# Buffer ownership, buffer hand-over points and pacing in a one-layer hybrid decoder trunk

## The chip, the cores and the metric

The kernel runs on one core of a Trainium2 chip. A core has a matrix engine (TensorE, PE in the profile; its weight loads are listed apart as PEld), a vector engine (DVE), a scalar engine (ACT), a general engine (POOL, GpSimd) and a sync engine (SP) that here only issues DMA transfers. Each engine runs its own instructions in order and waits on semaphores for the others. The metric is the device time of one execution in microseconds; the lower the better.

## What is computed

One decoder layer for 256 tokens of width 2048, all in 32-bit floats. The reference, cut to what matters:

```python
h = rmsnorm(x, attn_norm)
gq, gk, gv, gr, ga1, sq, sk, sv, mq, gates = split(h @ w_in)
# branch A: chunked gated linear attention, 4 heads, chunks of 64
log_a = log_sigmoid(ga1 @ w_a2 + b_a) / 16
y_gla = (rmsnorm(gla(gq, gk, gv, log_a)) * silu(gr)) @ w_br_gla
# branch B: causal stick-breaking attention, 8 heads of 128, 128-query blocks
y_sb = stick_breaking(rmsnorm(sq), rmsnorm(sk), sv) @ w_br_sb
# branch C: softmax cross-attention into 256 memory tokens, 4 heads of 256
m_k, m_v = split(rmsnorm(mem) @ w_mem_kv)
y_mem = softmax_attention(rmsnorm(mq), rmsnorm(m_k), m_v) @ w_br_mem
g = sigmoid(gates)
x = x + (g[0] * y_gla + g[1] * y_sb + g[2] * y_mem) @ w_o
gate, up = split(rmsnorm(x) @ w_gate_up)          # 2 x 5632 wide
out = x + (silu(gate) * up) @ w_down
```

## The kernel before

**Products.** Every weight matrix comes from memory in pieces of 1 MB (four 128-row slabs by 512 columns). Half a piece, called a chunk here, is split into a high and a low part: ACT rounds it to the matmul's type (`wh`, L145) and DVE subtracts to get the rest (`wl`, L146). Three matmuls per 128x128 block (high by high, high by low, low by high) then give nearly 32-bit products. A chunk is 12 full-size matmuls. `gemm` (L217 to L219) is the plain loop: 16 slabs are 8 chunks, 8 slabs are 4. `sgemm` (L256 to L259) computes two blocks of 512 columns together with a Strassen scheme on the first slabs; it also adds pieces in place, partly on DVE (L271) and partly by an accumulating DMA issued from POOL (L313, L333), and its intermediate results are copied out by ACT (L296). With p=4 it has 22 steps, of which 14 are steps of 6 matmuls and 8 are full chunks of 12; with p=2 it has 19, of which 7 have 6 matmuls and 12 have 12.

**Rings.** The 1 MB landing buffers stand in a list (`free_raw`); `loads` takes the first and the user puts it back at the end. The `wh`/`wl` buffers stand in another list (`splits`), and `parts` takes entry `turn % len(splits)`, where `turn` counts every chunk. `widen` appends a pool's buffers to both lists, `narrow` takes them out again. `ring1` lives throughout (3 landing buffers, 4 pairs of split buffers). `pre` adds one landing buffer, `ring_a` two landing buffers and two split pairs, and `ring2` three landing buffers and one split pair. `ring_a` lies where the normalised memory tokens (pool `mems`) were; `ring2` and `mrg` lie where the pools of the linear attention (`gl`, `att`, `sec`) were.

**Background.** Work that is not a product is written as generators in the list `background`. After each chunk a product calls `step`, which runs the first generator to its next `yield`; `flush` runs all that is left. `pipelined` makes such a generator from stages of several heads: in round r it runs the last stage for head r-2, the middle one for r-1 and the first for r, with a `yield` after each. The program order written down so is then the priority of a planner: on each engine the instruction that is ready first by the planner's own costs goes first, and program order decides between ready ones. The planner also chooses which of a tag's buffers a tile gets.

**The order of the stages.** Memory keys and values (four `gemm`s on `w_mem_kv`); `mq` in two `gemm`s of 512 columns; `sq`, `sk`, `sv` by `sgemm`, with the memory heads (`m_scores`, `m_turn`, `m_out`) in the background of `sq`; `gqk` and `gv` by `sgemm` with p=2, with the stick-breaking heads (`s_scores`, `s_rest`, `s_out`) in the background; `gr`, an `sgemm` whose result goes through a sigmoid; the small decay projection `w_ga`; then four rounds of a gate `gemm`, its sigmoid, the memory branch's product and `merge`, with the linear attention `gla` in the background; then the other two branches, `w_o` and the feed-forward part.

**Staged outputs.** The heads' results leave through `put_out` (L634 to L640): ACT copies PSUM into a tile of tag `rb`, which has two buffers and also holds the softmax's transposed scores (`m_turn`, L689) and the stick-breaking heads' `nl` (L760), and ACT's queue issues the store. `fetch_out` (L642) reads a whole branch back (1 MB) and splits it into `oh`, `ol` tiles (two steps, each with one split of 1024 columns).

Of the kernel before, what the change touches and what calls it, by code (L numbers as in the profile page):

```python
# [16 lines left out]
P = 128  # L17
# [60 lines left out]
def trunk(ctx: ExitStack, tc: tile.TileContext, a, out):  # L78
# [11 lines left out]
    def widen(name, raw, w, side="right"):  # L90

        pool = tc.alloc_tile_pool(name=name, bufs=1, side=side, reuse_waits="tile")
        free_raw.extend([(pool, raw)] * raw)
        splits.extend([(pool, w)] * w)
        return pool
# [20 lines left out]
    def tmp():  # L116
        return ps.tile([P, NB], F32, tag="tmp", name="tmp", bufs=4)
# [11 lines left out]
    def flush():  # L129
        while background:  # L130
            step()

    def pipelined(stages, n, gap):

        for r in range(n + gap * (len(stages) - 1)):
            for i in reversed(range(len(stages))):
                j = r - gap * i
                if 0 <= j < n:
                    stages[i](j)
                    yield  # L140

    def split(hi, lo, src, scale=None):

        if scale is None:
            act.copy(hi, src)  # L145
            dve.tensor_tensor(lo, src, hi.bitcast(F32), op=ALU.subtract)  # L146
        else:
            act.activation(hi, src, AF.Copy, scale=scale)
            dve.scalar_tensor_tensor(lo, src, scale, hi.bitcast(F32), op0=ALU.mult, op1=ALU.subtract)
# [19 lines left out]
    def loads():  # L169

        slot = pool, bufs = free_raw.pop(0)
        return pool.tile([P, KG, NB], F32, tag="raw", name="raw", bufs=bufs), lambda: free_raw.append(slot)

    def parts():

        turn[0] += 1
        pool, n = splits[turn[0] % len(splits)]
        return [pool.tile([P, IT], F32R, tag=f"w{x}", name=f"w{x}", bufs=n) for x in "hl"]
# [300 lines left out]
    def project(dst, xs, w, c0, rstd):  # L479
        for n in range(0, MIX, NB):  # L480
            evac(dst[:, :, n : n + NB], gemm(xs, w, c0 + n), rstd)
# [128 lines left out]

    pre = widen("pre", 1, 0, "left")
    opool.release()
    ring_a = widen("ring_a", 2, 2)

    def ring(tag, bufs, dtype=F32):
        return att.tile([P, NB], dtype, tag=tag, name=tag, bufs=bufs)
# [4 lines left out]
    def rb():  # L621
        return ring("rb", 2)
# [11 lines left out]

    def put_out(o, c, src):

        n = src.shape[1] // T
        v = rb()[:, : n * T]
        act.copy(v, src)
        nc.scalar.dma_start(o[:, c : c + n], v.rearrange("p (c t) -> p c t", c=n))  # L640

    def fetch_out(o):  # L642
        high, low = outT()

        def work():
            raw, done = loads()
            v = raw[:].rearrange("p g n -> p (g n)").rearrange("p (c t) -> p c t", c=8)
            nc.sync.dma_start(v, o[:])
            yield
            for c in range(0, 8, 4):  # L650
                split(high[:, c : c + 4], low[:, c : c + 4], v[:, c : c + 4])
                if c == 4:
                    done()
                yield

        background.append(work())
        return high, low
# [52 lines left out]

    sx = make_forms([xtiles], form_tiles())
    mq = section("mq", "d")
    project(mq, xs, w_in, O_MQ, r_x)
    flush()
    background.append(normed_T(mqT, mq, MH, MD, g_mq, ra))
    background.append(pipelined((m_scores, m_turn, m_out), MH, 1))
# [64 lines left out]
        put_out(od_sb, h, o[:, :T])  # L781

    flush()
    background.append(pipelined((s_scores, s_rest, s_out), SH, 1))
    gqk, gv = section("gqk", "a"), section("gv", "d")
    wide(gqk, O_GQ, 2)
    wide(gv, O_GV, 2)
# [9 lines left out]
            dve.tensor_tensor(v, v, sg, op=ALU.mult)  # L797
    narrow(ring_a)
    opool = tc.alloc_tile_pool(name="opool", bufs=4, side="right", reuse_waits="tile")
    o_mem, o_sb = fetch_out(od_mem), fetch_out(od_sb)  # L800


    narrow(pre)
    gl = tc.alloc_tile_pool(name="gl", bufs=1, reuse_waits="tile")
    raw, done = loads()
    raw = raw[:].rearrange("p g n -> p (g n)").rearrange("p (k n) -> p k n", k=KD)
    nc.sync.dma_start(raw, a["w_ga"])
    p = tmp()
    for k0 in range(0, KD, 8):
        hi, lo = (x[:].rearrange("p (k n) -> p k n", k=8) for x in parts())  # L810
        split(hi, lo, raw[:, k0 : k0 + 8])
        if k0 == 8:
            done()
        for j in range(8):
            xh, xl = xs[k0 + j]
            pe.matmul(p[:, :T], hi[:, j], xh, start=k0 + j == 0, stop=False)
            pe.matmul(p[:, :T], hi[:, j], xl, start=False, stop=False)
            pe.matmul(p[:, :T], lo[:, j], xh, start=False, stop=k0 + j == KD - 1)
    gaT = gl.tile([GR, T], F32, name="gaT", bufs=1)
    dve.tensor_copy(gaT[:], p[:GR, :T])  # L820
    flush()

    def gate():
        return piece()[:] if kit is not None else gl.tile([P, NB], F32, tag="sg", name="sg", bufs=2)[:]
# [112 lines left out]
                    )  # L937
                    yield

    background.append(gla())  # L940

    def to_chunks(src, n, hi, lo, gain):

# [31 lines left out]

    xo = pairs(o_mem)
    for n in range(0, D, NB):
        if n + NB == D:

            flush()  # L980
            gl.release()
            att.release()
            sec.release()
            ring2 = widen("ring2", 3, 1, "left")
            kit = mrg = tc.alloc_tile_pool(name="mrg", bufs=1, reuse_waits="tile")
        g = gemm(xs, w_in, O_G + n)
        sg = [gate() for _ in range(2)]
        for t in range(2):
            sigmoid(sg[t], g[t][:], t, False)
        merge(sg, gemm(xo, a["w_br_mem"], n), n, True)  # L990
# [170 lines left out]
```

## Time and profile before

| | us |
|---|---|
| median of 3 runs | 1655.15 |
| the runs | 1655.0, 1655.15, 1659.49 |
| the profiled execution | 1657.52 |
| its span, first to last instruction | 1655.7 |
| PE busy (share) | 1633.6 (99%) |
| DVE busy | 1308.4 (79%) |
| ACT busy | 1012.6 (61%) |

The span is what the trace covers; the profiled execution's own time is 1.8 us longer. A busy PE is not PE at its peak: the ends of matmuls are modelled, and the mean TensorE clock that was granted (0.994 over the span) is given by stretch. The profile's parts used here are the waits (who waited for whom, and how long), the busy times by stretch, the instructions in order of time, the groups by line, and the DMA transfers with the time from issue to landing.

### The profile page before, as it was taken

The page shows a single profiled execution, that of the slowest core. Times are in us where ns is not written, and L with a number is a line of the kernel's source. Part 1 is how long each engine was busy: PE and PEld are TensorE (multiplying, and loading weights), DVE is VectorE, ACT ScalarE, POOL GpSimd, SP SyncE. Part 2 cuts the span into 40 slices and gives each one's busy share as a digit, 9 for nine tenths or more (in the row PEclk, how much of TensorE's full clock was granted, in tenths as well). Part 3 has the DMA queues.
Part 4 walks back from the last instruction along what each step waited for, and adds up shares of the span by engine and source line. Part 5 has one row for each costly group of instructions (what it writes and reads, how often), then busy time and mean ns, then how long its engine had stood idle before and what let it go on. Part 6 is the DMA issues. An engine that isn't in the chain of part 4 may idle for free.

```text
span 1655.7 us, 19396 instructions
## 1 busy us (share of the span) xinstructions
PE 1633.6 (99%) x7290; PEld 1333.5 (81%) x7290; DVE 1308.4 (79%) x1506; ACT 1012.6 (61%) x1229; POOL 62.9 (4%) x81
## 2 busy tenths in 40 slices
PE   8999989999999999999999999999999999999999
PEld 6878878878887778888888888888888888888887
DVE  5857778877766557777787799999878999888994
ACT  6755566765745347556565666666666666666662
POOL 0000000000000000000000000000110000110000
PEclk9999999999999999999999999999999999999999
DMA  8785657657563367578585858787887687887792
GB/s 318 287 311 156 220 189 237 191 171 245 186 208 130 127 248 275 178 272 259 167 280 176 276 177 274 211 279 250 275 255 250 205 278 253 272 257 246 210 342 88
DMA packets 63006, 381.93 MB, mean 231 GB/s; under 512 B 6944, under 2 KB 12576, under 8 KB 19264
## 3 DMA queue, kind: packets, MB, share of 16 engines
q1 hardware_dynamic: 50256, 322.26, 51.7%
q0 software_dynamic: 10288, 55.58, 17.7%
q10 hardware_dynamic: 2368, 2.85, 0.5%
q8 instruction: 57, 0.93, 0.2%
q14 instruction: 37, 0.30, 0.1%
HBM read 322.99 MB, written 10.49 MB: 201 GB/s over the span
## 4 chain that ended last, share of the span: by engine, by line
PE 87%; DVE 3%; ACT 2%; DMA 1%; issue 1%; DVEq 0%; ACTq 0%
PE acc L256 17%; PE acc L259 17%; PE acc L258 16%; PE acc L218 6%; PE acc L219 6%; PE acc L217 6%; PE tmp L259 5%; PE tmp L256 5%; PE tmp L258 5%; PE tmp L435 2%; DVE wl L146 1%; ACT wh L145 1%; DMA od_mem<-rb 1%; PE tmp L904 0%; DMA od_sb<-rb 0%
## 5 line engine op out<-in xcount | busy, mean ns | idle before, releaser
L146 DVE TENSOR_TENSOR wl<-raw,wh 128x1024 fp32r<-128x1024 f32 (+1 forms) x740 | 891.7, 1219 | 274.2 <-ACT wh L145 261.4
L145 ACT CAST wh<-raw 128x1024 fp32r<-128x1024 f32 (+1 forms) x740 | 772.4, 1051 | 533.3 <-PE acc L259 247.1
L256 PE MATMUL acc<-wh,hh 128*128 128x512 f32 x452 | 178.8, 395 | 0.0
L258 PE MATMUL acc<-wl,hh 128*128 128x512 f32 x452 | 176.0, 389 | 0.0
L259 PE MATMUL acc<-wh,hl 128*128 128x512 f32 x452 | 175.4, 390 | 0.0
L256 PE MATMUL acc<-wh,xTh 128*128 128x512 f32 x424 | 170.1, 401 | 4.8 <-ACT acc L296 4.8
L258 PE MATMUL acc<-wl,xTh 128*128 128x512 f32 x424 | 166.7, 393 | 0.0
L259 PE MATMUL acc<-wh,xTl 128*128 128x512 f32 x424 | 166.0, 394 | 0.0
L271 DVE TENSOR_TENSOR raw<-raw 128x1024 f32<-128x1024 f32 x114 | 138.2, 1218 | 0.8
L217 PE MATMUL acc<-wh,oh 128*128 128x512 f32 x320 | 125.5, 394 | 1.9 <-ACT wh L145 1.1
L218 PE MATMUL acc<-wl,oh 128*128 128x512 f32 x320 | 124.9, 390 | 1.7 <-DVE wl L146 1.7
L219 PE MATMUL acc<-wh,ol 128*128 128x512 f32 x320 | 124.8, 390 | 0.0
L256 PEld LDWEIGHTS acc<-wh,hh 128*128 128x128 f32 x452 | 84.9, 188 | 18.4 <-ACT acc L296 1.0
L256 PEld LDWEIGHTS acc<-wh,xTh 128*128 128x128 f32 x424 | 80.3, 189 | 23.6 <-ACT acc L296 7.9
L259 PEld LDWEIGHTS acc<-wh,hl 128*128 128x128 f32 x452 | 84.8, 188 | 17.9
L258 PEld LDWEIGHTS acc<-wl,hh 128*128 128x128 f32 x452 | 85.0, 188 | 16.8
L256 PE MATMUL tmp<-wh,sh 128*128 128x512 f32 x246 | 97.3, 395 | 0.0
L259 PE MATMUL tmp<-wh,sl 128*128 128x512 f32 x246 | 96.0, 390 | 0.0
L258 PE MATMUL tmp<-wl,sh 128*128 128x512 f32 x246 | 95.8, 389 | 0.0
L259 PEld LDWEIGHTS acc<-wh,xTl 128*128 128x128 f32 x424 | 80.3, 189 | 17.0
L258 PEld LDWEIGHTS acc<-wl,xTh 128*128 128x128 f32 x424 | 80.4, 190 | 15.5
L217 PE MATMUL acc<-wh,xTh 128*128 128x512 f32 x192 | 76.7, 402 | 4.2 <-ACT wh L145 4.2
(313 smaller groups left out, 2526.4 us busy)
## 6 DMA issues: line engine op xcount, KB each, us to landing
raw<-in_w_gate_up SPq DMA_DIRECT2D x88, 1024.0 KB, 6.0
raw<-in_w_in SPq DMA_DIRECT2D x72, 1024.0 KB, 5.0
raw<-in_w_down SPq DMA_DIRECT2D x44, 1024.0 KB, 7.2
raw<-raw POOLq DMA_DIRECT2D x41, 1024.0 KB, 7.9
raw<-in_w_gate SPq DMA_DIRECT2D x32, 1024.0 KB, 5.9
raw<-in_w_o SPq DMA_DIRECT2D x16, 1024.0 KB, 5.3
raw<-in_w_mem_kv SPq DMA_DIRECT2D x15, 1024.0 KB, 5.0
raw<-in_w_br_mem SPq DMA_DIRECT2D x8, 1024.0 KB, 5.0
```

The costliest lines, as they stand in the source:

```text
L145: act.copy(hi, src)
L146: dve.tensor_tensor(lo, src, hi.bitcast(F32), op=ALU.subtract)
L217: pe.matmul(o[t][:], xh[:, s], wh[:, j], start=k == 0, stop=False)
L218: pe.matmul(o[t][:], xh[:, s], wl[:, j], start=False, stop=False)
L219: pe.matmul(o[t][:], xl[:, s], wh[:, j], start=False, stop=k == nk - 1)
L256: pe.matmul(dst[:], xh, wh, start=id(dst) not in begun, stop=False, skip_group_check=True)
L258: pe.matmul(dst[:], xh, wl, start=False, stop=False, skip_group_check=True)
L259: pe.matmul(dst[:], xl, wh, start=False, stop=last, skip_group_check=True)
L271: dve.tensor_tensor(x, x, y, op=ALU.add)
L435: pe.transpose(dst, src, ident)
```

## The change

Five things are edited; the arithmetic stays the same.

1. `put_out` gets its own tag `out` with two buffers of 256 columns. A memory head's result of 512 columns is copied and stored in two halves (8 copies and stores in place of 4); a stick-breaking head's in one, as before.
2. `ring_a` is made between the two halves of the `mq` projection, not before the first.
3. The stick-breaking heads get one empty step at the end of each round.
4. The linear attention's generator is made before the `w_ga` projection and its first step (two small loads) is run there. The read-back of the memory branch is put in the background behind `w_ga`, ahead of the rest of the linear attention, in place of both branches' read-backs before `w_ga` and a `flush` behind it.
5. In the last of the four gate rounds the gate's `gemm` comes first, and then the flush, the release of `gl`, `att` and `sec`, and the making of `ring2` and `mrg`. The read-back of the stick-breaking branch is started there.

```diff
-    def pipelined(stages, n, gap):
+    def pipelined(stages, n, gap, pause=False):
...
                     stages[i](j)
                     yield
+            if pause:
+                yield
...
     pre = widen("pre", 1, 0, "left")
     opool.release()
-    ring_a = widen("ring_a", 2, 2)
...
     def put_out(o, c, src):
 
-        n = src.shape[1] // T
-        v = rb()[:, : n * T]
-        act.copy(v, src)
-        nc.scalar.dma_start(o[:, c : c + n], v.rearrange("p (c t) -> p c t", c=n))
+        for i in range(src.shape[1] // T):
+            v = att.tile([P, T], F32, name="out", tag="out", bufs=2)
+            act.copy(v[:], src[:, i * T : (i + 1) * T])
+            nc.scalar.dma_start(o[:, c + i], v[:])
...
-    project(mq, xs, w_in, O_MQ, r_x)
+    evac(mq[:, :, :NB], gemm(xs, w_in, O_MQ), r_x)
+    ring_a = widen("ring_a", 2, 2)
+    evac(mq[:, :, NB:], gemm(xs, w_in, O_MQ + NB), r_x)
...
-    background.append(pipelined((s_scores, s_rest, s_out), SH, 1))
+    background.append(pipelined((s_scores, s_rest, s_out), SH, 1, True))
...
-    o_mem, o_sb = fetch_out(od_mem), fetch_out(od_sb)
...
-    (the w_ga projection, and gaT)
-    flush()
...
-    background.append(gla())
+    steps = gla()
+    next(steps)
+
+    (the w_ga projection, and gaT)
+    o_mem = fetch_out(od_mem)
+    background.append(steps)
...
     for n in range(0, D, NB):
+        g = gemm(xs, w_in, O_G + n)
         if n + NB == D:
 
             flush()
...
             ring2 = widen("ring2", 3, 1, "left")
             kit = mrg = tc.alloc_tile_pool(name="mrg", bufs=1, reuse_waits="tile")
-        g = gemm(xs, w_in, O_G + n)
+            o_sb = fetch_out(od_sb)
         sg = [gate() for _ in range(2)]
```

The two lines in brackets stand for the same lines, moved and not altered.

More of the change, by code (lines that the diff above doesn't have):

```diff
@@ L799, in trunk @@
     opool = tc.alloc_tile_pool(name="opool", bufs=4, side="right", reuse_waits="tile")
-    o_mem, o_sb = fetch_out(od_mem), fetch_out(od_sb)
     narrow(pre)
     gl = tc.alloc_tile_pool(name="gl", bufs=1, reuse_waits="tile")
[L805 to L820, printed above, removed]
-    flush()
     def gate():
@@ L938, in gla_T @@
                     yield
-    background.append(gla())
+    steps = gla()
+    next(steps)
+    raw, done = loads()
+    raw = raw[:].rearrange("p g n -> p (g n)").rearrange("p (k n) -> p k n", k=KD)
+    nc.sync.dma_start(raw, a["w_ga"])
+    p = tmp()
+    for k0 in range(0, KD, 8):
+        hi, lo = (x[:].rearrange("p (k n) -> p k n", k=8) for x in parts())
+        split(hi, lo, raw[:, k0 : k0 + 8])
+        if k0 == 8:
+            done()
+        for j in range(8):
+            xh, xl = xs[k0 + j]
+            pe.matmul(p[:, :T], hi[:, j], xh, start=k0 + j == 0, stop=False)
+            pe.matmul(p[:, :T], hi[:, j], xl, start=False, stop=False)
+            pe.matmul(p[:, :T], lo[:, j], xh, start=False, stop=k0 + j == KD - 1)
+    gaT = gl.tile([GR, T], F32, name="gaT", bufs=1)
+    dve.tensor_copy(gaT[:], p[:GR, :T])
+    o_mem = fetch_out(od_mem)
+    background.append(steps)
     def to_chunks(src, n, hi, lo, gain):
```

## The prediction

> **What bounds the kernel now.** I read the page's busy times, then the waits of PE, then the busy times by stretch around those waits, then the instructions in order of time on the engines that PE waited for.
>
> ```profile
> span 1655.7 us, 19396 instructions
> PE 1633.6 (99%) x7290; PEld 1333.5 (81%) x7290; DVE 1308.4 (79%) x1506; ACT 1012.6 (61%) x1229; POOL 62.9 (4%) x81
> ...
> PE acc L217 <- ACT wh L145: 5.3, 3, 2.1
> PE acc L256 <- ACT acc L296: 4.8, 2, 4.5
> PE acc L218 <- DVE wl L146: 3.4, 6, 0.9
> PE tmp L779 <- DVE ra L774: 1.6, 1, 1.6
> ...
> L146 DVE TENSOR_TENSOR wl<-raw,wh 128x1024 fp32r<-128x1024 f32 (+1 forms) x740 | 891.7, 1219 | 274.2 <-ACT wh L145 261.4
> L145 ACT CAST wh<-raw 128x1024 fp32r<-128x1024 f32 (+1 forms) x740 | 772.4, 1051 | 533.3 <-PE acc L259 247.1
> ```
>
> PE bounds the kernel, and the edits take no matmul away. All that can be won is where PE waited (1655.7 - 1633.6 = 22.1 us) and where its clock was low. The rows by stretch (columns: stretch, its length, PE busy and matmuls, PEld, DVE, ACT, POOL, then granted clock, DMA share, GB/s) price the places:
>
> ```profile
> 95.00:105.00 10.00, 7.39 (x32) 5.48 (x31) 6.76 (x11) 6.94 (x8) 0.00 (x0) 1.00 0.86 342
> 205.00:225.00 20.00, 15.53 (x56) 12.21 (x56) 12.15 (x21) 10.97 (x15) 0.00 (x0) 0.83 0.33 122
> 330.00:340.00 10.00, 8.43 (x40) 6.59 (x39) 7.42 (x13) 7.00 (x12) 0.00 (x0) 1.00 0.88 317
> 445.00:460.00 15.00, 14.22 (x72) 11.40 (x72) 12.33 (x17) 12.79 (x20) 0.00 (x0) 0.89 0.76 259
> 575.00:592.00 17.00, 14.05 (x49) 10.77 (x48) 10.13 (x14) 4.92 (x6) 0.00 (x0) 0.80 0.75 304
> 700.00:1000.00 300.00, 300.00 (x1353) 247.70 (x1352) 242.47 (x275) 176.79 (x212) 11.88 (x17) 1.00 0.69 232
> ```
>
> The waits list who waited for whom (total, times, longest); the two groups give one split of a chunk, 1.05 on ACT and 1.22 on DVE. The last row by stretch is undisturbed: a chunk of 12 matmuls is 12 x 300/1353 = 2.7 us. In the others, idle is length less PE busy, and the loss by the clock is length times (1 - clock). A: 10 - 7.39 = 2.6 us. B: 4.5 + 20 x 0.17 = 7.9, less some 0.4, an estimate, for low clock that began before PE's wait ended, 7.5. C: 1.6. D: 0.8 + 15 x 0.11 = 2.4. E: 2.95 + 17 x 0.20 = 6.35, less the same 0.4, 6.0. Together 20.1 us; each edit has one of these places as its own.
>
> **Edit 2, `ring_a` one block on (place A).** Chunks are counted by `turn`: the memory projections use 33 (their first `gemm` begins with pieces of 1, 1 and 2 slabs, so 9, then three times 8). The first chunk of `mq` is number 34. With `ring_a` in the list there are 6 entries, and 34 mod 6 = 4 is `ring_a`'s, whose place is free only when the last memory product has read it. In order of time (start, duration, engine, line, idle before it and who ended that):
>
> ```profile
> 97.19 2.00 ACT L145 CAST wh<-raw 128x1024 fp32r<-128x1024 f32 x2 [4.60 <-DMA raw<-in_w_in]
> 99.09 1.26 ACT L477 ACTIVATE mv_mqT<-acc,r_mem 128x512 f32<-128x512 f32 x2
> 100.24 3.89 ACT L145 CAST wh<-raw 128x1024 fp32r<-128x1024 f32 x4
> ```
>
> Two later chunks are rounded at 97.19; the first comes after the evacuation, at 100.24, and PE waits for it. With the list of four, 34 mod 4 = 2 is a `ring1` buffer, and ACT sat idle for 4.60 us before 97.19. The second block starts at 42 mod 6 = 0, a `ring1` buffer, and reaches `ring_a` 4 chunks later, at least 4 + 8 chunks after it came free. What is late next is the landing of the pieces: those two chunks themselves waited for a DMA until 97.19, some 1.9 us before PE needs the first (100.24 + 3.89/4, less the 2.1 that PE waited), against 1.05 and 1.22 for a split. I take -2.6; bounds -2.6 and 0.
>
> **Edit 5, the pools behind the last gate (place E).** `turn` goes on: 16 for `mq`, 22 each for `sq`, `sk`, `sv`, 19 each for `gqk`, `gv`, 22 for `gr`, 2 for `w_ga`, three rounds of 8 + 4. The last gate's first chunk is number 214. With `ring2` there are 5 entries and 214 mod 5 = 4 is `ring2`'s, in memory that the linear attention holds until its last operation (L920, which reads `gr`):
>
> ```profile
> 578.96 1.21 DVE L920 TENSOR_TENSOR g_og<-g_og,gr 128x1024 f32<-128x1024 f32 x1
> ...
> 579.45 1.99 ACT L145 CAST wh<-raw 128x1024 fp32r<-128x1024 f32 x2 [1.66 <-PE acc L219]
> ...
> 581.50 0.73 PE L217 MATMUL acc<-wh,xTh 128*128 128x512 f32 x2 [2.08 <-ACT wh L145]
> 583.10 0.80 PE L218 MATMUL acc<-wl,xTh 128*128 128x512 f32 x1 [0.87 <-DVE wl L146]
> ```
>
> The second of the two casts at 579.45 starts when L920 ends (580.17); PE starts when it ends. Moved, the last gate runs on `ring1` alone like the three gates before it, in which PE shows no such wait, and its 8 chunks (some 21 us) lie between L920 and the first use of `ring2`. The linear attention ends two steps later than now (three steps of read-back ahead of it, one of its own already done), so L920 comes up to 5.4 us later, still inside that cover. It then falls among the last gate's first subtractions on DVE (1.2 each), whose chunks are split ahead of PE. The read-back of `od_sb` moves into the last branch product: 2 casts and 2 subtractions of 1.0 and 1.2, hidden by its 4 chunks; without that cover 2.4 us. `ring2`'s landing buffers join a gate later, so loads of the next gate weights run less far ahead: 0 to +3. I take -6.0; bounds -6.3 and -1.
>
> **Edit 4, `w_ga` and the read-backs (place D).**
>
> ```profile
> 424.77 0.33 SPq L648 DMA_DIRECT2D raw<-od_mem  x1
> 435.76 0.33 SPq L648 DMA_DIRECT2D raw<-od_sb  x1
> ...
> 440.22 3.90 ACT L145 CAST oh<-raw 128x1024 fp32r<-128x1024 f32 x4 [2.54 <-PE acc L259]
> ...
> 450.24 1.03 ACT L145 CAST wh<-raw 128x1024 fp32r<-128x1024 f32 x1
> ...
> 450.52 1.12 PE L837 MATMUL tmp<-rb,gaT 16*128 16x512 f32 x2 [0.51 <-DVE gaT L820]
> ```
>
> SP now issues both read-backs ahead of the first gate's pieces, and ACT rounds `oh` from 440.22 to 444.1; the first gate's first cast comes behind `gr`'s sigmoid at 450.24, when PE has nothing left of `w_ga`. Afterwards the first gate piece is issued where `od_mem` stands (424.77), and its cast fits into the ACT time that `oh` has now; the second buffer pair is free when `gr`'s last chunk ends. `od_mem` takes the second issue and is split in steps 2 and 3. The decay's first matmuls (L837) no longer stand between `w_ga` and the gate: their 1.1 us are moved, not saved. What is late next is the second chunk, behind the same sigmoid. I take -2.0; bounds -2.4 and +2 (if the cast stays behind the sigmoid, PE lacks the 1.1 us that it fills now, and the low clock of that place, 15 x 0.11, stays or grows).
>
> **Edits 1 and 3, the stick-breaking heads (place C).** Where `nl` got the buffer of a store in flight, DVE waited 2.0 us and PE 1.6:
>
> ```profile
> DVE rb L760 <- DMA od_sb<-rb: 2.0, 1, 2.0
> ...
> od_sb<-rb ACTq DMA_DIRECT2D x8, 128.0 KB, 2.7
> ```
>
> With its own two buffers a store has two rounds to land, 17 us at the 8.6 us between issues (312.8 to 373.3 for 8, in the rows by tile below), against 6.6 at worst. `nl` never meets a store. The 10 empty steps bring 24 steps to 34; the two projections give 2 x 19 = 38, so all stay covered. -1.6; bounds -2.5 (ACT's crowding where `gqk` is evacuated) and +0.5 where the heads' end now meets `gv`'s evacuation.
>
> **Edit 1, the memory heads (place B).** Here I expect little.
>
> ```profile
> L640 ACTq DMA_DIRECT2D od_mem<-rb x4: 326/334/353, 178.5 to 208.6; - x4
> ...
> DMA to landing us min/median/max: 2.5/5.7/9.1
> ...
> L640 ACTq DMA_DIRECT2D od_sb<-rb x8: 326/326/1954, 312.8 to 373.3; - x8
> ...
> DMA to landing us min/median/max: 1.9/2.7/6.6
> ...
> 197.46 0.85 POOL L333 DMA_DIRECT2D raw<-raw  x1 [35.90 <-DVE ra L680]
> ...
> 208.02 0.58 ACT L639 COPY rb<-tmp 128x512 f32<-128x512 f32 x1 [5.15 <-DMA od_mem<-rb]
> 213.81 0.57 ACT L296 COPY acc<-tmp 128x512 f32<-128x512 f32 x1
> 214.44 0.80 PE L256 MATMUL acc<-wh,xTh 128*128 128x512 f32 x1 [4.47 <-ACT acc L296]
> ```
>
> The last head's copy waits for the store before it (issued 198.84, landed 9.1 us later, behind the 1 MB accumulating transfer issued at 197.46); ACT stands, and its queue holds up the casts and the copy L296 for which PE waits. Two buffers for two halves of each head is the same distance as before: the first half still waits for the head before it. The store is no smaller in all, only cut, and ACT issues 0.33 us more and starts one more copy per head, hidden but at the last. Bounds: halves that land like `od_sb`'s median, 2.7, would take the stall away (-7.5); a second half that lands behind a further load costs up to about +2.5. I take +0.5, since the row nearest is the 9.1 of this very store.
>
> The Trainium skill, page "DMA: Bandwidth & Descriptors", section "Anatomy of one DMA — SWDGE (gpsimd) path", speaks against the cut too: a transfer has a fixed part of about 2.0 us that does not scale with its size, so halving 256 KB saves only some 0.3 us by its formula, an estimate. The trace's medians, 5.7 against 2.7, fall by more, but in other stretches; by the page's figure place B would come out at +0.2.
>
> **The sum.** -2.6 - 6.0 - 2.0 - 1.6 + 0.5 = -11.7. The profiled execution took 1657.5 (its span and 1.8 us around it), which becomes 1645.8; it stood 2.4 above the median of the runs, 1655.15, from which I go: 1643.5.
>
> **Rivals.**
>
> *The store stall goes as well.* The planner may give the halves their buffers otherwise, or the shift of everything by A's 2.6 us may part the store from the accumulating transfer. For it: the four stores' landings spread from 2.5 to 9.1. Against it: the accumulation and the store hang on the same heads' steps. 1643.5 - 0.5 - 7.5 = 1635.5.
>
> *New lateness eats half.* Loads that run less far ahead behind `ring2` (+3), the cast behind the sigmoid (+4 against my term) and the ends of the heads (+2): up to 9, say half, 1648. For it: the chunks before the last gate are split only when PE frees a buffer (1.66 before 579.45).
>
> *The low clock has another cause.* If it does not come from PE's idle time, the low clock at D and E stays: 15 x 0.11 + 17 x 0.20 - 0.4 = 4.6, so 1648. For it: 2.6 us of idle at A left the clock at 1.00, while 0.8 at D went with 0.89. Against it: outside these stretches the clock is 1.00 where PE is never idle. The Trainium skill, page "TensorE: Matmul & The Clock Gate", section "What's actually happening", lowers the clock after an idle window of some 3.4 us; by that rule only B's wait would bring a low clock, and D and E agree with it badly.
>
> *It does not do what it says.* The planner orders by readiness, so each wait could come back one block on: 1655. Against it: the buffers have been free for whole blocks by then.
>
> *Slower: the paced heads outrun their cover.* If the two projections had fewer than 34 steps, the rest would run in the flush with nothing beside it.
>
> ```profile
> L756 ACT ACTIVATE ra<-tmp 128x384 f32<-128x384 f32 x8 | 3.8, 481 | 0.4 <-PE tmp L754 0.4
> ...
> L760 DVE SCALAR_TENSOR_TENSOR rb<-tmp,ra 128x384 f32<-128x384 f32 x8 | 4.4, 554 | 2.8 <-DMA od_sb<-rb 2.0 <-ACT ra L758 0.9
> L772 DVE TENSOR_TENSOR ra<-ra,tmp 128x384 f32<-128x384 f32 x8 | 4.4, 552 | 5.0 <-PE tmp L771 5.0
> ```
>
> The first stage of a head is a chain of four such ACT and four DVE operations, about 4 x 0.5 + 4 x 0.5 + 0.6 on PE = 4.6; ten steps are 2.5 rounds, 11.5; the last head's two other stages some 4, and a low clock behind it like B's 3.4: +19, or 1662.5. It decides from the 35th step that is needed; I count 38 there.
>
> **How the numbers follow.** My forecast 0.48, with 1639 to 1648 as its own range; the store stall gone 0.18; new lateness 0.14; the clock 0.06; nothing changed 0.08; slower 0.06. About 0.3%, 5 us, is what a measurement of this kernel can tell from no change. Faster: 0.48 + 0.18 + 0.14 + 0.06 = 0.86; within 0.08; slower 0.06. The range 1634 to 1651 takes in the first four cases.
>
> **What would show it.** Right: no wait of L217 near 99 and 579 us, and clock 1.00 at D and E; DVE L760 never released by a store; a copy L639 in `mq`'s heads still released by `od_mem`, with L296 and a low clock behind it. Wrong: a new wait of PE on `wh` or `wl` at the second `mq` block, the last branch product or the end of `gv`; or a trace in which L639 waits for no store.

## The result, and the profile after

The changed kernel takes 1637.38 us (median of 4 runs, 1636.86 to 1638.47), the kernel before beside it 1655.08 (1654.84 to 1659.49). The ratio is 0.9888 with a 95% interval of 0.987 to 0.9905: faster by 17.7 us, where the prediction had 11.7 and 1643.5. The time lies in the predicted range, below the likeliest case's own range (1639 to 1648) and next to the rival in which the store stall goes as well (1635.5).

Line numbers are 2 to 4 higher now: the splits are L148 and L149, the products L220 to L222 and L259 to L262, the copy out of `sgemm` L299, `put_out` L641 and L642. The linear attention's are 16 lower: its last operation, L920 before, is L904. First the page of the kernel after, span and busy times.

```profile
span 1634.9 us, 19398 instructions
PE 1625.0 (99%) x7290; PEld 1330.8 (81%) x7290; DVE 1308.6 (80%) x1506; ACT 1014.5 (62%) x1233; POOL 62.9 (4%) x81
```

The span is 20.8 us shorter, but PE's waits shrank only from 22.1 to 9.9 us. The rest is PE busy time, 8.6 us less for the same 7290 matmuls: they ran at a higher clock or back to back. So the busy times by stretch have to say where the time came from. Before:

```profile
0.00:90.00 90.00, 85.21 (x368) 66.91 (x369) 64.80 (x116) 63.27 (x92) 0.20 (x4) 1.00 0.83 298
90.00:190.00 100.00, 97.15 (x440) 79.23 (x438) 66.80 (x98) 56.23 (x75) 1.89 (x2) 1.00 0.68 234
190.00:295.00 105.00, 100.26 (x447) 81.94 (x446) 85.26 (x112) 68.06 (x86) 4.11 (x5) 0.97 0.67 217
295.00:395.00 100.00, 97.89 (x451) 79.83 (x450) 73.51 (x96) 65.33 (x97) 2.76 (x4) 1.00 0.61 189
...
430.00:460.00 30.00, 29.22 (x141) 23.95 (x141) 22.80 (x27) 22.83 (x31) 0.00 (x0) 0.94 0.58 200
460.00:560.00 100.00, 100.00 (x447) 77.31 (x445) 59.87 (x85) 44.19 (x62) 1.05 (x2) 1.00 0.48 167
560.00:600.00 40.00, 37.05 (x146) 28.55 (x146) 21.96 (x38) 16.99 (x26) 0.00 (x0) 0.91 0.53 207
600.00:1000.00 400.00, 400.00 (x1800) 329.83 (x1799) 317.93 (x352) 236.27 (x281) 14.81 (x20) 1.00 0.68 227
```

And after, the same stretches (columns as in the prediction: length, PE busy and matmuls, PEld, DVE, ACT, POOL, granted clock, DMA share, GB/s):

```profile
0.00:90.00 90.00, 87.52 (x373) 69.55 (x374) 66.27 (x117) 64.85 (x93) 0.20 (x4) 1.00 0.83 302
90.00:190.00 100.00, 99.77 (x454) 82.06 (x453) 68.50 (x101) 58.26 (x79) 1.89 (x2) 1.00 0.72 243
190.00:295.00 105.00, 102.06 (x465) 83.18 (x464) 89.73 (x116) 72.74 (x95) 4.26 (x5) 1.00 0.71 221
295.00:395.00 100.00, 99.83 (x466) 83.26 (x465) 77.98 (x100) 67.81 (x99) 3.46 (x4) 1.00 0.63 195
...
430.00:460.00 30.00, 30.00 (x157) 25.10 (x155) 20.73 (x25) 21.19 (x30) 0.53 (x1) 1.00 0.60 205
460.00:560.00 100.00, 100.00 (x440) 75.93 (x441) 59.24 (x88) 46.18 (x69) 0.53 (x1) 1.00 0.44 149
560.00:600.00 40.00, 40.00 (x179) 33.10 (x178) 30.88 (x46) 22.45 (x29) 0.86 (x1) 1.00 0.76 276
600.00:1000.00 400.00, 400.00 (x1803) 329.61 (x1802) 324.74 (x360) 239.69 (x285) 14.82 (x20) 1.00 0.71 233
```

The count of matmuls in a stretch reads idle time and clock in one: a matmul more in the same stretch is 400/1803 = 0.222 us of work done earlier. It is rough where a border shifts small matmuls from one stretch to the next, as at 460, so D is read over 430 to 560.

| place | matmuls more | gain in us | gain forecast |
|---|---|---|---|
| start, 0 to 90, no edit | 5 | 1.1 | 0 |
| A, 90 to 190 (`ring_a`) | 14 | 3.1 | 2.6 |
| B, 190 to 295 (memory heads) | 18 | 4.0 | -0.5 |
| C, 295 to 395 (stick-breaking heads) | 15 | 3.3 | 1.6 |
| D, 430 to 560 (`w_ga`) | 16 - 7 = 9 | 2.0 | 2.0 |
| E, 560 to 600 (last gate) | 33 | 7.3 | 6.0 |
| sum | 94 | 20.8 | 11.7 |

The sum is the difference of the spans. By medians it is 17.7: the profiled execution of before stood 2.4 above its median and that of after 0.5 below. The start is no part of the change. Behind 600 us the two kernels run alike (1803 and 1800). So the forecast was about right at A, D and E, half at C, and the largest piece that it lacked is B, 4.5 of 9.1 us. What PE still waits for (total, times, longest):

```profile
PE acc L259 <- ACT acc L299: 1.9, 1, 1.9
PE tmp L561 <- DVE zeros L558: 1.2, 1, 1.2
PE tmp L698 <- ACT rb L691: 0.8, 1, 0.8
```

The first and third stand at B; the second is at the kernel's first matmuls, as are two more of 0.7 and 0.5 us. The store wait at B is smaller, not gone. The transfers of `od_mem` after, by tile (the issue on ACT with its shortest, median and longest time in ns, and the landing):

```profile
L642 ACTq DMA_DIRECT2D od_mem<-out x8: 326/365/1993, 174.0 to 202.9; - x8
...
DMA to landing us min/median/max: 2.7/4.3/7.5
```

The same place in order of time, ACT's instructions, with idle time and releaser in brackets:

```profile
194.51 2.41 ACTq L642 DMA_DIRECT2D od_mem<-out  x2
196.97 0.58 ACT L691 COPY rb<-tmp 128x512 f32<-128x512 f32 x1 [2.21 <-PE acc L262]
...
202.10 0.65 ACT L641 COPY out<-tmp 128x256 f32<-128x256 f32 x2 [2.03 <-DMA od_mem<-out]
```

The wait that was 5.15 us is 2.03, on the same buffer reuse the prediction named. The landing fell from 9.1 to 7.5, which is 1.6 of the 3.1. The other 1.5 is that ACT came to the next head's copy later: before, it began to wait 4.0 us after the store's issue (208.02 - 5.15 - 198.84), now 5.6 (202.10 - 2.03 - 194.51). This part is a shorter wait but no time won by itself. One of the two issues at 194.51 held ACT for 1.99 us, and the copy of `rb` for which PE waited 0.8 us stands right behind it.

### The profile page after: what moved, and what is told of

Same layout as the page of the kernel before. It is cut to its first block, busy times and chain, and to the rows that moved or that the text cites. A ratio compares the mean times of both kernels' runs of the same rounds, so it can differ in the third digit from the quotient of the medians.

```text
span 1634.9 us, 19398 instructions
## 1 busy us (share of the span) xinstructions
PE 1625.0 (99%) x7290; PEld 1330.8 (81%) x7290; DVE 1308.6 (80%) x1506; ACT 1014.5 (62%) x1233; POOL 62.9 (4%) x81
## 4 chain that ended last, share of the span: by engine, by line
PE 97%; DMA 1%; ACT 1%; DVE 1%; issue 0%; ACTq 0%; DVEq 0%
PE acc L259 17%; PE acc L262 17%; PE acc L261 17%; PE acc L220 8%; PE acc L221 8%; PE acc L222 8%; PE tmp L259 6%; PE tmp L262 6%; PE tmp L261 5%; PE tmp L438 2%; DMA od_mem<-out 0%; DVE wl L149 0%; DMA raw<-in_w_mem_kv 0%; PE tmp L888 0%; ACT wh L148 0%; PE tmp L883 0%
## 5 line engine op out<-in xcount | busy, mean ns | idle before, releaser
L149 DVE TENSOR_TENSOR wl<-raw,wh 128x1024 fp32r<-128x1024 f32 (+1 forms) x740 | 892.4, 1221 | 259.9 <-ACT wh L148 246.5
L148 ACT CAST wh<-raw 128x1024 fp32r<-128x1024 f32 (+1 forms) x740 | 772.5, 1051 | 511.8 <-PE acc L262 237.9
L259 PE MATMUL acc<-wh,hh 128*128 128x512 f32 x452 | 178.8, 396 | 0.0
L262 PE MATMUL acc<-wh,hl 128*128 128x512 f32 x452 | 175.4, 390 | 0.0
L259 PE MATMUL acc<-wh,xTh 128*128 128x512 f32 x424 | 169.0, 399 | 2.1 <-ACT acc L299 1.9
L262 PE MATMUL acc<-wh,xTl 128*128 128x512 f32 x424 | 165.3, 391 | 0.0
L220 PE MATMUL acc<-wh,oh 128*128 128x512 f32 x320 | 126.4, 397 | 0.8 <-ACT oh L151 0.7
L222 PE MATMUL acc<-wh,ol 128*128 128x512 f32 x320 | 125.5, 392 | 0.0
L259 PEld LDWEIGHTS acc<-wh,hh 128*128 128x128 f32 x452 | 84.9, 188 | 18.5 <-ACT acc L299 1.0
L262 PEld LDWEIGHTS acc<-wh,hl 128*128 128x128 f32 x452 | 84.8, 188 | 17.8
L259 PE MATMUL tmp<-wh,sh 128*128 128x512 f32 x246 | 97.3, 396 | 0.0
L259 PEld LDWEIGHTS acc<-wh,xTh 128*128 128x128 f32 x424 | 79.6, 188 | 20.5 <-ACT acc L299 4.6
L262 PE MATMUL tmp<-wh,sl 128*128 128x512 f32 x246 | 96.1, 391 | 0.0
L262 PEld LDWEIGHTS acc<-wh,xTl 128*128 128x128 f32 x424 | 79.6, 188 | 16.9
L220 PE MATMUL acc<-wh,xTh 128*128 128x512 f32 x192 | 75.5, 394 | 0.0
```

The lines of the kernel that those rows point to most:

```text
L220: pe.matmul(o[t][:], xh[:, s], wh[:, j], start=k == 0, stop=False)
L222: pe.matmul(o[t][:], xl[:, s], wh[:, j], start=False, stop=k == nk - 1)
L259: pe.matmul(dst[:], xh, wh, start=id(dst) not in begun, stop=False, skip_group_check=True)
L262: pe.matmul(dst[:], xl, wh, start=False, stop=last, skip_group_check=True)
```

## The experiments

My theory after the result: each edit does at its own place what the prediction says, and at B the cut into halves shortens the store's landing. Rivals: the shift of everything by A's gain parts the store from the accumulating transfer (then undoing edit 2 brings the long landing back); the own tag gives B its gain (then whole stores in a buffer of their own keep it); or the gain at B is an accident of the held issue. Every kernel below is the changed kernel with the edit shown, and a time stands against 1637.38 unless another is named. The runs lie on several chips; the kernel before, run beside them, had medians of 1654.05 to 1656.8. Medians of two such kernels within 2 us are not told apart here, so the place is read from its stretch and the median is the second witness.

**Edit 2 undone.**

```diff
     opool.release()
+    ring_a = widen("ring_a", 2, 2)
...
-    evac(mq[:, :, :NB], gemm(xs, w_in, O_MQ), r_x)
-    ring_a = widen("ring_a", 2, 2)
-    evac(mq[:, :, NB:], gemm(xs, w_in, O_MQ + NB), r_x)
+    project(mq, xs, w_in, O_MQ, r_x)
```

> The changed kernel with edit 2 taken back: ring_a is in the list from the first mq chunk on. Theory (the first chunk falls on ring_a's split pair, whose memory the last memory product still reads): PE waits again for wh at the start of mq, 2.6 us between 95 and 105, the clock stays 1.00, and the time is 1640.0 (1637.4 + 2.6). Rival 1 (the gain in this place came from the cut stores or another edit): no wait there, 1637.4. Rival 2 (the memory heads' store wait shrank because everything came 2.6 us earlier and so met the accumulating transfer differently): the memory heads' copy waits over 5 us for its store again, PE waits 4.5 there with a low clock behind it, and the time is about 1644.5.

Measured: 1642.36 us (1641.82 to 1643.29), ratio to before 0.991 (0.9894 to 0.9926), so 5.0 slower than the changed kernel. A's stretch, PE's wait for the first chunk of `mq`, and the issue and landing of `od_mem`:

```profile
95.00:105.00 10.00, 7.76 (x26) 5.68 (x25) 6.99 (x6) 7.05 (x8) 0.00 (x0) 0.83 0.83 328
...
PE acc L220 <- ACT wh L148: 1.7, 1, 1.7
...
L643 ACTq DMA_DIRECT2D od_mem<-out x8: 326/361/2611, 178.4 to 207.7; - x8
...
DMA to landing us min/median/max: 2.6/3.3/7.9
```

The idle time of A comes back (2.24 us), and this time a low clock with it (0.83), which the same place did not have before. The landing stays short (7.9), and the heads' stretch, 190 to 295, holds 465 matmuls as in the changed kernel. The shift by A is not what B gained.

**Edit 5 undone, edit 4 kept.**

```diff
-        g = gemm(xs, w_in, O_G + n)
         if n + NB == D:
 
             flush()
...
             ring2 = widen("ring2", 3, 1, "left")
             kit = mrg = tc.alloc_tile_pool(name="mrg", bufs=1, reuse_waits="tile")
+        g = gemm(xs, w_in, O_G + n)
+        if n + NB == D:
             o_sb = fetch_out(od_sb)
```

> The changed kernel with the pools of edit 5 made ahead of the last gate's gemm again (the read-back of the stick-breaking branch stays behind it). Theory (chunk 214 falls on ring2's split pair, held until the linear attention's last multiplication, and the wait lowers the clock): that multiplication now ends some 2.7 to 5.4 us later than before, so PE waits 3 to 8 us at the last gate's first chunk, low clock (under 0.85 over 17 us) behind it, time 1643 to 1648. Rival (the low clock there has another cause than PE's idle time): the wait returns, the clock stays 1.00, time 1640 to 1645. Rival (edit 5 gave nothing, the linear attention's new place did): under 1639.

Measured: 1648.9 us (1647.57 to 1650.95), ratio 0.995 (0.9932 to 0.9967), 11.5 slower than the changed kernel. The stretch of E (the changed kernel has 143 matmuls and clock 1.00 in it), then ACT, DVE and PE in order of time:

```profile
560.00:592.00 32.00, 24.29 (x93) 19.02 (x92) 18.70 (x34) 11.42 (x16) 0.00 (x0) 0.84 0.61 233
...
566.01 1.99 ACT L148 CAST wh<-raw 128x1024 fp32r<-128x1024 f32 x2 [1.30 <-PE acc L222]
...
572.00 1.22 DVE L904 TENSOR_TENSOR g_og<-g_og,gr 128x1024 f32<-128x1024 f32 x1
573.14 1.22 DVE L149 TENSOR_TENSOR wl<-raw,wh 128x1024 fp32r<-128x1024 f32 x1
...
568.05 0.73 PE L220 MATMUL acc<-wh,xTh 128*128 128x512 f32 x2 [2.08 <-ACT wh L148]
574.41 0.79 PE L221 MATMUL acc<-wl,xTh 128*128 128x512 f32 x1 [5.63 <-DVE wl L149]
```

PE comes to the last gate at 566.0, waits 2.08 us for the chunk's cast, and then 5.63 for its subtraction, which starts only when the linear attention's last operation (L904) ends, at 573.2. So the last operation holds the chunk up, as the prediction said, but through the subtraction: the cast that PE waits for is done at 568.0, five microseconds before L904 ends. The place lost 50 matmuls, 11.1 us, against 7.3 that it gave back between before and after. The difference is edit 4, which puts the linear attention later: the wait for the subtraction was 0.87 in the kernel before, 4.8 less. By these counts edit 4 without edit 5 loses more at E (11.1 - 7.3 = 3.8) than it wins at D (2.0).

**Edit 4 undone, edit 5 kept.**

```diff
-    steps = gla()
-    next(steps)
-
+    o_mem, o_sb = fetch_out(od_mem), fetch_out(od_sb)
     (the w_ga projection, and gaT)
-    o_mem = fetch_out(od_mem)
-    background.append(steps)
+    flush()
+    background.append(gla())
...
-            o_sb = fetch_out(od_sb)
```

> The changed kernel with edit 4 taken back: both branches are read back ahead of w_ga, flushed behind it, and the linear attention starts after that. Theory (the first gate's first cast stands behind the read-back splits and the sigmoid of gr): the cast comes when w_ga's matmuls have ended, PE waits 0.8 us and runs at low clock for 3 us, time 1639.8 (+2.4). The linear attention also ends two steps earlier. Rival (the read-backs were hidden, what counted is where the decay's first matmuls stand): L837's successors still fill, under +1, clock 1.00. If the low clock does not come with the wait, +0.8.

Measured: 1639.88 us (1637.76 to 1642.38), ratio 0.9895 (0.9876 to 0.9914); the profiled span is 1636.0, 1.1 more than after's. By medians that is 2.5 slower, but the runs spread over 4.6 us and the profiled one is the fastest of them.

```profile
430.00:460.00 30.00, 29.22 (x151) 24.19 (x150) 23.12 (x29) 22.45 (x32) 0.53 (x1) 1.00 0.66 230
```

The idle time of D is back to the hundredth (0.78 us, as before). The low clock is not: 1.00 here, 0.94 in this stretch of the kernel before. So of the 2.0 us of D, 0.8 are surely the edit's. The low clock behind the same idle time comes in one kernel and not in the other.

**Edit 3 undone.**

```diff
-    background.append(pipelined((s_scores, s_rest, s_out), SH, 1, True))
+    background.append(pipelined((s_scores, s_rest, s_out), SH, 1))
```

> The changed kernel without the empty step per round of the stick-breaking heads; the stores keep their own buffers. Theory (place C's gain comes from the stores' own buffers, the pacing adds little): no wait of DVE L762 for a store, PE within 0.7 us of the changed kernel between 295 and 395, time 1637.9 (+0.5). Rival (the pacing is what took the wait away, since a store had more time to land and ACT and DVE more room): PE waits 1.5 us or more there, time 1639 to 1640.

Measured: 1638.48 us (1638.05 to 1640.24), ratio 0.9888 (0.9869 to 0.9908).

```profile
295.00:395.00 100.00, 99.67 (x459) 81.53 (x458) 76.00 (x98) 65.37 (x96) 3.47 (x4) 1.00 0.60 193
```

With own buffers and no pacing no instruction of the heads waits for a store, so that suffices for the wait of `nl`. Still the stretch holds 7 matmuls less than after's 466, 1.6 us, and the span is 1.9 longer: the crowded heads cost something without one long wait.

**Edit 1 undone: whole stores, in the shared tag.**

```diff
-        for i in range(src.shape[1] // T):
-            v = att.tile([P, T], F32, name="out", tag="out", bufs=2)
-            act.copy(v[:], src[:, i * T : (i + 1) * T])
-            nc.scalar.dma_start(o[:, c + i], v[:])
+        n = src.shape[1] // T
+        v = rb()[:, : n * T]
+        act.copy(v, src)
+        nc.scalar.dma_start(o[:, c : c + n], v.rearrange("p (c t) -> p c t", c=n))
```

> The changed kernel with edit 1 taken back: outputs are staged whole in rb again, shared with the scores and nl; the other four edits stay. Theory 1 (the cut into halves, each with its own buffer, is what let the last memory head's copy start earlier): its copy waits about 5 us for the store again, PE waits 4 to 5 there with a low clock behind, and a DVE wait for a store among the stick-breaking heads may come back; time 1642 to 1645. Theory 2 (the stall shrank because the other edits moved the stores against the accumulating transfer): the copy's wait stays at 1.6 to 2.0 us and the time is within 1 us of 1637.4.

Measured: 1640.4 us (1636.11 to 1644.74), ratio 0.9904 (0.987 to 0.9937). By medians 3.0, with a spread that wide not decided; the profiled run (1640.24) is 3.3 longer in span and shows where:

```profile
190.00:295.00 105.00, 100.52 (x449) 82.18 (x448) 86.74 (x114) 69.44 (x87) 4.28 (x5) 0.97 0.68 214
295.00:395.00 100.00, 99.79 (x466) 83.20 (x465) 77.50 (x98) 68.14 (x100) 3.47 (x4) 1.00 0.62 197
...
  ACT rb L641: 4.9, 1
...
PE acc L259 <- ACT acc L299: 4.2, 1, 4.2
```

B is back as it was before: 449 matmuls for 465 (16 x 0.222 = 3.6 us), ACT's 4.9, PE's 4.2, the clock. And C is not: 466 matmuls, as after, although the stick-breaking heads store from the tag that `nl` uses. With the pacing the shared tag does no harm there.

**Own tag, uncut.** One buffer of 512 columns, as many bytes as the two halves.

```diff
-        for i in range(src.shape[1] // T):
-            v = att.tile([P, T], F32, name="out", tag="out", bufs=2)
-            act.copy(v[:], src[:, i * T : (i + 1) * T])
-            nc.scalar.dma_start(o[:, c + i], v[:])
+        n = src.shape[1] // T
+        v = ring("out", 1)[:, : n * T]
+        act.copy(v, src)
+        nc.scalar.dma_start(o[:, c : c + n], v.rearrange("p (c t) -> p c t", c=n))
```

> The changed kernel with whole stores through one own buffer of 512 columns, the same bytes of SBUF as the two halves. If the cut is what counts, the last memory head's copy waits about 5 us for the 256 KB store (issue to landing 7 to 9) and PE 4 to 5, time 1641 to 1645. If being apart from rb is what counts, the wait stays at about 2 us and the time at 1637 to 1639. The long issue of a store (2.0 to 2.6 us on ACT's queue in the runs so far, once per run) is there in both, if it comes from the second of two stores close behind each other it is gone here. A stick-breaking head's store has one round to land, 8.6 us or more against 5.1 at worst, so no wait there.

Measured: 1641.44 us (1639.75 to 1641.87), ratio 0.9908 (0.989 to 0.9925), 4.1 slower.

```profile
190.00:295.00 105.00, 100.35 (x448) 82.04 (x447) 86.58 (x114) 68.14 (x86) 4.28 (x5) 0.97 0.68 215
...
DMA to landing us min/median/max: 2.5/4.8/9.0
```

The own tag alone gives B nothing (448 matmuls). What gained there is the cut, with what came with it. (This kernel also lost 6 matmuls in its first 90 us, before any edit: 367 against 373.)

**Whole stores at two heads' distance.** If distance is what counts, as the prediction argued against the halves, then four halves' worth of buffers must take the wait away. The tag `rc` has two buffers of 512 columns that stand idle meanwhile.

```diff
-        for i in range(src.shape[1] // T):
-            v = att.tile([P, T], F32, name="out", tag="out", bufs=2)
-            act.copy(v[:], src[:, i * T : (i + 1) * T])
-            nc.scalar.dma_start(o[:, c + i], v[:])
+        n = src.shape[1] // T
+        if n == 1:
+            v = att.tile([P, T], F32, name="out", tag="out", bufs=2)[:]
+        else:
+            v = att.tile([P, NB], F32, name="rc", tag="rc", bufs=2)[:]
+        act.copy(v, src)
+        nc.scalar.dma_start(o[:, c : c + n], v.rearrange("p (c t) -> p c t", c=n))
```

> The changed kernel with the memory heads' outputs staged whole in the two rc buffers, which nothing uses in that stage; the stick-breaking heads keep the halves' tag. A memory head's store now has two heads' time to land. Theory (place B's rest is the distance of one head): no ACT wait for od_mem, PE's wait for L299 gone and the loss between 190 and 225 down by 2 to 3.5 us, time 1634 to 1635.5. Rival (ACT would be late there anyway, by the copies and casts it has in that stretch): the wait for the store goes but PE waits as long for L299, time 1637.

Measured: 1633.78 us (1633.45 to 1634.23), ratio 0.9863 (0.9847 to 0.9879).

```profile
190.00:295.00 105.00, 104.87 (x479) 86.15 (x478) 92.65 (x121) 74.72 (x95) 4.28 (x5) 1.00 0.71 224
...
L645 ACTq DMA_DIRECT2D od_mem<-rc x4: 326/329/353, 175.1 to 200.2; - x4
...
DMA to landing us min/median/max: 3.9/5.7/7.5
```

No instruction waits for a store, PE is idle for 0.13 us of 105, and the stretch holds 14 matmuls more than after's (3.1 us). Against the kernel before that is 32 matmuls, 7.1 us, close to the 7.5 at which the prediction priced the whole place. No issue is held either (353 ns at most). This is a better kernel than the changed one; the comparison on one chip is below.

**The same, with the stick-breaking heads back in `rb`, without and with the pacing.** The `put_out` of both is the last one with one line changed; the first has edit 3 undone as well.

```diff
         if n == 1:
-            v = att.tile([P, T], F32, name="out", tag="out", bufs=2)[:]
+            v = rb()[:, :T]
...
-    background.append(pipelined((s_scores, s_rest, s_out), SH, 1, True))
+    background.append(pipelined((s_scores, s_rest, s_out), SH, 1))
```

> The kernel of e8 (memory heads staged whole in rc, 1633.8) with the stick-breaking heads as they were at first: staged in rb, shared with nl, and no empty steps. Theory of the prediction (the store in flight in rb held DVE up): DVE L764 waits for a store of od_sb for some 2 us, PE 1.6 us, time 1636 to 1637.5. Rival (the wait was an accident of where the loads stood, as the store's landing of 6.6 then): no wait for a store, only the small losses of the unpaced heads, about +1.3, time 1635.

> The kernel of e8 with the stick-breaking heads staged in rb again, but paced. Theory after the runs so far (the empty steps alone give the store its time, the own buffers add nothing): no wait for a store, time within 0.5 us of 1633.8, and the tag out is not needed. Rival (both are needed): a wait of DVE for a store, time 1635 to 1636.

Measured: without the pacing 1637.15 us (1636.08 to 1639.69), ratio 0.9894 (0.9876 to 0.9911); with it 1634.48 (1634.34 to 1635.28), ratio 0.9876 (0.9861 to 0.9892). Without:

```profile
295.00:395.00 100.00, 98.33 (x453) 80.22 (x452) 74.53 (x95) 65.51 (x96) 3.47 (x4) 1.00 0.62 191
...
DVE rb L767 <- DMA od_sb<-rb: 1.7, 1, 1.7
```

With:

```profile
295.00:395.00 100.00, 99.83 (x466) 83.31 (x465) 78.14 (x98) 67.19 (x97) 3.47 (x4) 1.00 0.65 202
```

With neither own buffers nor pacing the wait of before is back (13 matmuls, 2.9 us). The pacing alone takes all of it away; the own buffers alone (edit 3 undone, above) take the wait but leave 1.6 us. So C was won by the pacing, and the own buffers for these heads are not needed beside it.

The stores of `od_mem` in the paced version also separate distance from landing:

```profile
DMA to landing us min/median/max: 3.5/5.8/9.8
```

One of them took 9.8 us, longer than the 9.1 of the kernel before, and still nothing waited for it.

**The second half stored from SP's queue.** This keeps the cut and its buffers and takes the second issue, the one that held ACT, away from ACT.

```diff
-            nc.scalar.dma_start(o[:, c + i], v[:])
+            (nc.sync if i else nc.scalar).dma_start(o[:, c + i], v[:])
```

> The changed kernel, with the second half of each memory head stored by SP's queue and not by ACT's. It tells why the halves land sooner. Theory 1 (half the bytes ahead of the half that is waited for): the first half lands within 7.0 to 7.9 us, ACT is not held by a long issue (all under 0.4 us), PE's wait for rb L691 (0.8 to 1.5 us) goes, time 1636 to 1637. Theory 2 (the long second issue holds ACT's casts and so pushes the next load away from the store): the load is issued some 2.7 us behind the store again, the half lands in about 9 us, ACT waits 4 us or more for it, time 1640 to 1642.

Measured: 1639.32 us (1638.12 to 1639.98), ratio 0.9902 (0.9883 to 0.9921), 1.9 slower than the changed kernel.

```profile
190.00:295.00 105.00, 101.64 (x458) 83.09 (x457) 88.37 (x116) 70.11 (x91) 4.26 (x5) 0.98 0.70 220
...
  ACT out L641: 4.1, 1
...
DMA to landing us min/median/max: 2.5/3.7/8.3
```

The next load of a weight piece, as SP's queue issued it, in this kernel and in the changed one:

```profile
198.49 0.33 SPq L253 DMA_DIRECT2D raw<-in_w_in  x1
```

```profile
199.78 12.20 SPq L253 DMA_DIRECT2D raw<-in_w_in  x2
```

This lies between the two theories. The cut without the held issue brings part of B's gain: the landing falls from 9.0 (own tag, uncut) to 8.3, and B holds 458 matmuls against 448, 2.2 us. The other 7 matmuls of the changed kernel, 1.6 us, go with the held issue: there the next 1 MB load leaves 5.3 us after the store (199.78 - 194.51) and not 2.9 (198.49 - 195.60), and the store lands 0.8 us sooner. That the later load is what lets it land sooner was not isolated, and neither it nor the cut is needed for 7.5: in the `rc` version the whole store issued at 195.48 has the next load 2.7 us behind it (198.18), and its longest landing is 7.5 too. For most of the 1.6 us the rows point to the clock: it is 0.98 here against 1.00, which over 105 us is 2.1, while PE's idle time differs by 0.4 (3.36 and 2.94). Here PE waits 3.4 us in one piece, in the changed kernel 1.9 and 0.8 apart.

**The changed kernel and the `rc` version on one chip, five rounds.**

> The changed kernel itself, beside e13 on one chip: 1636.5 to 1638.5, as in its first runs.

> The kernel of e8 beside the changed one on one chip, to see whether it is faster by more than the runs spread. Theory: 3 to 4 us under e12 (the rest of the memory heads' store wait, 2.0 of ACT's wait and the store's held issue), with no overlap of the two spreads. Rival (the difference lay between chips and calls): within 1 us of e12.

Measured: the changed kernel 1638.9 us (1636.93 to 1640.07), ratio 0.9906 (0.9889 to 0.9923); the `rc` version 1634.33 (1633.13 to 1635.11), ratio 0.9879 (0.986 to 0.9897). They do not overlap, 4.6 us apart, of which the counts at B explain 3.1. The first 90 us of the changed kernel in this second profile, no edit being there:

```profile
0.00:90.00 90.00, 85.25 (x365) 67.78 (x366) 64.95 (x116) 63.84 (x92) 0.20 (x4) 0.98 0.81 295
```

365 matmuls, where the first profile of the very same kernel has 373 and the kernel before has 368. Its clock of 0.98 is a loss of that size (90 x 0.02 = 1.8). The start varies by 8 matmuls, 1.8 us, by itself, so the 1.1 us in the table's first row are no part of the change.

## Why the prediction was right or wrong

**A, `ring_a`: right.** The turn arithmetic named the buffer, and undoing the edit brings the wait back at that very chunk. Measured 3.1 for 2.6. Worth 5.0 by medians when undone, since a low clock joined it there.

**E, the pools: right, with its cover.** Forecast 6.0, measured 7.3. The last gate runs on `ring1` without a wait, and PE waits for nothing behind 560 us. One reading was wrong: the second of the two casts at 579.45 does not start when L920 ends (580.17) but when the cast before it does (579.45 + 1.99/2, some 580.4), and with edit 5 undone it ran five microseconds before the last operation ended. So, as far as the rows show, 2.08 us of PE's wait came from the order of two casts on ACT, and only the 0.87 behind them from the linear attention. Edit 5 removes both; why the planner put that cast second is not shown. "The linear attention ends two steps later than now" held too, and the experiment shows what the sentence was worth: without edit 5 those steps cost 3.8 us more than in the kernel before. The bound of 0 to +3 for loads running less far ahead measured 0 (1803 matmuls against 1800 from 600 to 1000 us).

**D, `w_ga`: right in sum** (2.0 and 2.0), half shown. The idle 0.8 is the edit's. The low clock that I priced at 15 x 0.11 did not return with the idle time.

**C, the stick-breaking heads: the wait was right, its remedy only half.** The forecast of 1.6 priced the one wait; measured 3.3. The step "With its own two buffers a store has two rounds to land" is true, but the pacing, to which I gave only a cover count, also removes the wait on its own and takes away 1.6 us of crowding that the waits do not list as one item. The slower rival, paced heads that outrun their cover, did not come: the last store is issued at 381.4 and no idle time follows.

**The bounds.** A, C and E gave more than the most I allowed (3.1 for 2.6, 3.3 for 2.5, 7.3 for 6.3), all the same way. At C it is the crowding; at A and E the reason is open. The whole range held because it took in the rival in which the store stall goes, not because the likeliest case came.

**B, the memory heads: the wrong term.** The step that failed is "I take +0.5, since the row nearest is the 9.1 of this very store". Its first half, that two halves of a buffer are the same distance, was right: the wait is still there (2.03), and doubling the distance is what removes it. Wrong was to carry the landing over unchanged and to let ACT's cost outweigh the rest. The cut store landed in 7.5, ACT came to the next head's copy 1.5 us later, and PE's wait fell from 4.5 to 1.9, after which the clock stayed at 1.00. PE's idle time in the stretch fell by 1.8 us (4.74 to 2.94); the larger part of the 4.0 is the low clock, which did not come. ACT's cost did come, and larger than priced: one issue took 1.99 us where I had 0.33, and PE waited 0.8 behind it. I had written the bounds -7.5 and +2.5, and chose a point close to the wrong end. The long landing was no accident that any shift mends: with whole stores in a buffer of their own and all other edits it was 9.0 again.

The Trainium skill, page "DMA: Bandwidth & Descriptors", section "Anatomy of one DMA — SWDGE (gpsimd) path", gave some 0.3 us for halving the store, as the prediction estimated; its formula is for transfers that GpSimd issues, and these stores are issued by ACT. The run with the second half on SP's queue shows 0.7 (9.0 to 8.3), but whole stores landed in 7.5 and in 9.8 at this place in the `rc` versions, so one store does not settle a difference of this size. The larger part of B's gain is not in that formula.

**The rivals.** *The store stall goes as well*: half of it came, 4.0 of its 7.5 us, by neither of the reasons I gave for it. *New lateness*: none. *The low clock has another cause*: rejected in sum, since with the idle times the low clock went from B, D and E; but it does not follow the idle time one to one.

## What to carry to other kernels

When a ring gets new buffers, count which use lands on the new one first and who still holds its memory, and let it join where that use comes after the holder's end. A staging buffer that waits for its own store needs distance: a second full buffer from an idle tag took the wait away, cutting the store in two only shortened it. Undo edits one at a time before crediting them: one that starts work later (edit 4) can be a gain only beside another (edit 5) that moves what depends on its end.

## What the hardware showed that I had not expected

**An issue on ACT's queue that takes 2 us.** Most stores are issued in 0.33 us. The second of the two halves that ACT issued about 1.6 us after POOL's accumulating transfer took 1.99 us in the changed kernel; the longest issue of `od_mem` was 2.61 with edit 2 undone and 1.88 in the changed kernel's second profile.

The changed kernel's accumulating transfer, on POOL's queue:

```profile
193.35 0.85 POOL L336 DMA_DIRECT2D raw<-raw  x1 [36.03 <-DVE ra L682]
```

The single whole store of the other versions, at the same place, took 0.35 at most. It need not be a second half: in the kernel before, POOL issued an accumulating transfer at 371.81, ACT a load at 372.92 (0.34 us), and the store of a stick-breaking head that ACT issued next, at 373.31, took 1.95. ACT stands for the time of its issue. Why the second issue is held was not settled.

**A short idle time and the clock.** PE's idle time at a place and the clock granted there: 2.6 us and 1.00 (A before), 2.24 and 0.83 (A with edit 2 undone), 0.78 and 0.89 (D before), 0.78 and 1.00 (D with edit 4 undone). The length of the idle time alone does not decide. Where the clock is low it is about half: in the kernel before, the matmuls at E start 0.43 us apart from 583.7 to 588.8, and 0.23 apart behind that. The Trainium skill, page "TensorE: Matmul & The Clock Gate", section "What's actually happening", has the clock fall after an idle window of some 3.4 us that runs free of the kernel's start. That the same idle time ends both ways would agree with a window that runs free; that 0.78 us went with a low clock at all does not agree with the length.
